# A hybrid decoder trunk on one core: the gated MLP with PSUM chains, seeded down products and one plain pair per layer

## The chip, the core and the metric

The kernel runs on one core of a Trainium2 chip. The time is device microseconds of one launch. Five queues work beside each other and wait for each other through semaphores: TensorE (PE; its weight loads are PEld), VectorE (DVE), ScalarE (ACT), GpSimd (POOL) and SyncE (SP, which here only issues loads from memory). Each works through its own instructions in order.

## The reference

Two layers on 512 tokens of 1024 channels. Layer 0 mixes tokens with a gated recurrence and a pooling branch, layer 1 with a convolution module; each layer then attends to 256 memory tokens and ends with the gated MLP that is changed here. All of it is float32.

```
def conv_ffn(x, norm, w_up, dw_w, dw_b, w_down):
    h = rms_norm(x, norm) @ w_up                       # 1024 -> 2 x 3072
    g = causal_dwconv(h[..., :D_FF], dw_w, dw_b)       # 3 taps along the tokens
    u = h[..., D_FF:]
    return (jax.nn.gelu(g) * u) @ w_down               # 3072 -> 1024
x = x + conv_ffn(...)
```

## The kernel before

Activations stay in SBUF, channels on the partitions and the 512 tokens along a row; the residual is eight tiles X. Every float32 product is three matmuls (mm3): each operand is split into a high part (ScalarE copies it rounded to float32r) and a low part (VectorE subtracts), and high x high, high x low and low x high are summed in PSUM. So each weight block costs a copy on ACT (method high) and a subtraction on DVE (method low).

**The MLP (function ffn, once per layer).** The 3072 hidden channels are 24 chunks of 128. A chunk needs two projections, gate and value: a pair. It is computed in one of two ways.

- *Plain:* two products, each 8 blocks x 3 matmuls of 512 tokens (48 matmuls). The first three chunks are plain (PLAIN = 3), in function opening.
- *Seven products (Strassen's scheme in Winograd's form):* gate and value are the two rows of a 2 x 2 block product, the token halves (256 tokens each) its columns, the channel halves the inner index. Seven products of 4 blocks x 3 matmuls of 256 tokens (84 matmuls) replace eight. The token side (B11, B21, B22 and sums T1 to T4) is made once per layer by class Seven, in four parts; the last part is made in opening. The weight side (a11, a12, a22 and sums s1 to s4) is made per chunk in class Blocks: GpSimd issues DMAs that accumulate within SBUF, on a tile r and a tile z. low() issues each one right behind the low part that last read the tile: r += z after a11, z += a22 after a22, r += a22 after s3, r += a12 after s2. z += a22 has to wait until r += z has landed. s1 is read from z; s3, s2, s4 from r, in this order.

**Function unit(c)** does one chunk: the products in the order a11, a12, s2, s3, s1, s4, a22, each into a PSUM bank of its own (pool of five), then VectorE adds them up (m1, u2, u3, u4, f, g), seven adds of 256 tokens and one copy on ACT. gating() then scales by the norm, convolves three taps, applies gelu, multiplies gate and value and splits the result into ys[c]; it is a generator, so that its later steps are written between the next chunk's. Between the products stand the high and low parts of the next chunks' blocks and the loads (chunk c + 3's first tile, c + 2's second).

**Down products.** The second projection goes in six groups of four chunks. While group g + 1 is computed, each unit does two of the eight output tiles of group g (class Down, 12 matmuls of 512 tokens each, into one of two aux banks); VectorE then adds the bank to X (sum, line 836). The first units of a layer, up to chunk 3, have no down product.

**Function opening** runs the plain chunks. start(0) is the first plain product; then the norm's mean on PE, its root on ACT with a table load, its reciprocal on DVE (scale_of), further plain products, and between them the preparation of the first seven-product chunks (first and second) and the last part of the token sums.

**What sets the order.** Inside ffn the four engines PE, ACT, DVE and POOL run in the order in which the code is written (manual_schedule); SP's loads are placed by a scheduler, which also orders the code around ffn. Each queue waits at its own head: an instruction that waits for a DMA holds up all that is behind it on its engine.

## Time and profile before

| what | value |
|---|---|
| median of 3 runs | 1430.96 us (1429.98 to 1431.38) |
| profiled execution, span | 1429.2 us |
| PE busy, matmuls | 1418.0 us, 99%, 8578 |
| DVE busy | 1184.4 us, 83% |
| ACT busy | 800.7 us, 56% |
| POOL busy | 311.2 us, 22% |
| DMA | 202.23 MB, mean 141 GB/s |

The profile is of one execution. Lines L... are lines of the kernel. "out<-in" names the tile that is written and those that are read; mm and aux are PSUM banks, whi and wlo the high and low parts of weights, raw and wa the tiles that weights are loaded to, bigr other split operands, act split activations. In a timeline a row is start, length, engine, line, operation; in square brackets stands how long the engine sat idle before it, and what ended that. PE's matmuls overlap, so a stage's cost is read from the distance between starts, or from a window that holds whole products. In layer 0 the MLP's first plain product starts at 355.03 us and the first chunk of seven products at 388.16 us.

### The profile page before, as it was taken

The page shows a single profiled execution, that of the slowest core. Times are in us where ns is not written, and L with a number is a line of the kernel's source. Part 1 is how long each engine was busy: PE and PEld are TensorE (multiplying, and loading weights), DVE is VectorE, ACT ScalarE, POOL GpSimd, SP SyncE. Part 2 cuts the span into 40 slices and gives each one's busy share as a digit, 9 for nine tenths or more (in the row PEclk, how much of TensorE's full clock was granted, in tenths as well). Part 3 has the DMA queues.
Part 4 walks back from the last instruction along what each step waited for, and adds up shares of the span by engine and source line. Part 5 has one row for each costly group of instructions (what it writes and reads, how often), then busy time and mean ns, then how long its engine had stood idle before and what let it go on. Part 6 is the DMA issues. An engine that isn't in the chain of part 4 may idle for free.

```text
span 1429.2 us, 22885 instructions
## 1 busy us (share of the span) xinstructions
PE 1418.0 (99%) x8578; PEld 1259.4 (88%) x8578; DVE 1184.4 (83%) x1980; ACT 800.7 (56%) x1336; POOL 311.2 (22%) x325
## 2 busy tenths in 40 slices
PE   9999999999999999999999999999999999999998
PEld 7988888998899999999988777899889999999997
DVE  6987776778888888888888997978788988888885
ACT  7678754666644444544555547767665444444434
POOL 0011310200122221222008992010012222221201
PEclk9999999999999999999999999999999999999999
DMA  8523232542577777777432454345247876877741
GB/s 302 197 74 104 89 119 80 118 111 89 136 183 169 172 181 165 164 176 169 140 119 89 118 158 153 105 87 148 86 114 162 178 184 157 171 183 159 164 127 60
DMA packets 78591, 202.23 MB, mean 141 GB/s; under 512 B 8848, under 2 KB 9360, under 8 KB 78480
## 3 DMA queue, kind: packets, MB, share of 16 engines
q1 hardware_dynamic: 50544, 150.15, 33.6%
q0 software_dynamic: 27648, 50.34, 21.3%
q8 instruction: 67, 1.10, 0.3%
q14 instruction: 44, 0.36, 0.1%
q10 hardware_dynamic: 288, 0.27, 0.1%
HBM read 145.16 MB, written 2.10 MB: 103 GB/s over the span
## 4 chain that ended last, share of the span: by engine, by line
PE 90%; DVE 3%; DMA 2%; POOL 2%; issue 1%; ACT 1%; SPq 0%; POOLq 0%; DVEq 0%; ACTq 0%
PE mm L187 22%; PE mm L186 22%; PE mm L188 22%; PE aux L186 7%; PE aux L187 7%; PE aux L188 7%; PE mm L458 2%; DMA raw<-in_wv 1%; DVE wlo L167 1%; POOL actf L1469 1%; ACT whi L166 1%; PE aux L531 0%; POOL act L167 0%; POOL tmp L1290 0%; DMA raw<-in_pw 0%
## 5 line engine op out<-in xcount | busy, mean ns | idle before, releaser
L187 PE MATMUL mm<-act,whi 128*128 128x512 f32 (+2 forms) x1077 | 377.1, 350 | 0.6 <-DVE act L181 0.5
L188 PE MATMUL mm<-act,wlo 128*128 128x512 f32 (+2 forms) x1077 | 376.7, 350 | 0.0
L186 PE MATMUL mm<-act,whi 128*128 128x512 f32 (+2 forms) x1077 | 376.6, 351 | 0.0
L187 PEld LDWEIGHTS mm<-act,whi 128*128 128x128 f32 x1077 | 203.7, 189 | 29.0 <-DVE act L167 1.0
L186 PEld LDWEIGHTS mm<-act,whi 128*128 128x128 f32 x1077 | 203.4, 189 | 28.4 <-ACT tmp L1468 0.8
L188 PEld LDWEIGHTS mm<-act,wlo 128*128 128x128 f32 x1077 | 203.6, 189 | 25.8
L797 ACT ACTIVATE bigr<-raw 128x512 fp32r<-128x512 f32 x168 | 105.6, 628 | 166.8 <-DMA raw<-wa 70.4
L188 PE MATMUL mm<-bigr,bigr 128*128 128x256 f32 x672 | 190.2, 283 | 0.0
L187 PE MATMUL mm<-bigr,bigr 128*128 128x256 f32 x672 | 190.2, 283 | 0.0
L186 PE MATMUL mm<-bigr,bigr 128*128 128x256 f32 x672 | 190.0, 283 | 0.0
L171 DVE TENSOR_TENSOR tmp<-mm,tmp 128x256 f32<-128x256 f32 x336 | 136.3, 419 | 31.6 <-PE mm L188 25.9
L186 PE MATMUL aux<-act,whi 128*128 128x512 f32 x399 | 156.3, 392 | 0.0
L187 PE MATMUL aux<-act,whi 128*128 128x512 f32 x399 | 156.2, 391 | 0.0
L188 PE MATMUL aux<-act,wlo 128*128 128x512 f32 x399 | 155.2, 389 | 0.0
L804 DVE TENSOR_TENSOR bigr<-raw,bigr 128x512 fp32r<-128x512 f32 x168 | 115.5, 688 | 37.0 <-ACT bigr L797 34.8
L166 ACT ACTIVATE whi<-raw 128x1024 fp32r<-128x1024 f32 (+1 forms) x95 | 96.4, 1019 | 84.1 <-PE mm L187 44.0
L187 PEld LDWEIGHTS mm<-bigr,bigr 128*128 128x128 f32 x672 | 128.9, 192 | 1.6
L186 PEld LDWEIGHTS mm<-bigr,bigr 128*128 128x128 f32 x672 | 128.9, 192 | 1.5
L188 PEld LDWEIGHTS mm<-bigr,bigr 128*128 128x128 f32 x672 | 128.9, 192 | 0.0
L807 POOL DMA_DIRECT2D raw<-raw x48 | 41.6, 866 | 343.1 <-DVE wlo L804 283.3
L811 POOL DMA_DIRECT2D raw<-wa x48 | 41.5, 864 | 308.3 <-DVE bigr L804 258.5
L167 DVE TENSOR_TENSOR wlo<-raw,whi 128x1024 fp32r<-128x1024 f32 (+1 forms) x75 | 90.5, 1210 | 20.0 <-ACT whi L166 19.8
(351 smaller groups left out, 3026.1 us busy)
## 6 DMA issues: line engine op xcount, KB each, us to landing
raw<-wa POOLq DMA_DIRECT2D x144, 256.0 KB, 4.6
wa<-in_wpair SPq DMA_DIRECT2D x84, 256.0 KB, 3.5
raw<-in_wpair SPq DMA_DIRECT2D x42, 512.0 KB, 5.7
big<-in_wdown SPq DMA_DIRECT2D x42, 512.0 KB, 6.7
raw<-raw POOLq DMA_DIRECT2D x48, 256.0 KB, 7.6
raw<-in_pw SPq DMA_DIRECT2D x24, 512.0 KB, 3.4
raw<-in_win SPq DMA_DIRECT2D x20, 512.0 KB, 3.4
raw<-in_wk SPq DMA_DIRECT2D x16, 512.0 KB, 3.6
```

The costliest lines, as they stand in the source:

```text
L166: A.activation(hi, src, AF.Copy)
L167: fetched[1] = (eng or V).tensor_tensor(lo, src, hi.bitcast(F32), op=ALU.subtract)
L171: V.tensor_tensor(out, a, b, op=ALU.add)
L186: PE.matmul(ps, wh, xh, start=first, stop=False)
L187: PE.matmul(ps, wh, xl, start=False, stop=False)
L188: PE.matmul(ps, wl, xh, start=False, stop=last)
L458: PE.matmul(p, m[j], x, start=k == 0 and j == 0 and x is hi, stop=k == C - 1 and x is lo)
L797: A.activation(self.w[name][0], self.block(name), AF.Copy)
L804: V.tensor_tensor(lo, self.block(name), hi.bitcast(F32), op=ALU.subtract)
L807: G.dma_start(self.r, self.z, accum_op=ALU.add)
L811: G.dma_start(self.r, self.a22, accum_op=ALU.add)
L1469: G.tensor_tensor(z[:, s:], z[:, s:], f[:, s:], op=ALU.add)
```

## The change

The weights for one chunk instead of three are laid out plainly (PLAIN = 1), so each layer has 23 chunks of seven products instead of 21.

In a unit the products accumulate in three PSUM banks instead of being added on VectorE. G starts with a11. ScalarE copies G into F (function ahead, done for the next chunk before the present one ends). F then takes s2, s3 and a22, and is copied to SBUF after each; G takes a12; H starts with s1 and takes s4. The order is s1, s2, a12, [down half], s3, [down half], the next chunk's a11, a22, s4. Two adds remain on VectorE. A down half starts on a bank into which ScalarE has copied X, accumulates onto it, and is copied back to X by ScalarE (from chunk 5 on). The opening has two plain products.

```
-PLAIN = 3
+PLAIN = 1
...
-    def mm3(ps, w, x, first, last):
+    def mm3(ps, w, x, first, last, onto=False):
...
+            def bank(self, i, seeded):
+                ps = aux_ps()
+                if seeded:
+                    A.activation(ps, X[2 * self.j + i], AF.Copy)
+                return ps
+            def home(self, i, ps, seeded):
+                if seeded:
+                    A.activation(X[2 * self.j + i], ps, AF.Copy)
+                else:
+                    self.sum(i, ps)
...
-            add(f[:, :M], ps, u3)
+            A.activation(f[:, :M], F, AF.Copy)
+            add(g[:, M:], H, u[:, :M])
...
+        def ahead(c):
+            G, F = main_ps()[:, :M], main_ps()[:, :M]
+            m(c, G, "a11", seven.B11)
+            A.activation(F, G, AF.Copy)
+            return G, F
         def unit(c):
+            G, F = chains
+            down, seeded = downs.get(c), c > GC
+            H = main_ps()[:, :M]
+            m(c, H, "s1", seven.T1)
+            if down:
+                d0 = down.bank(0, seeded)
+            high(c + 1, "s3")
+            m(c, F, "s2", seven.T2, False)
+            u, f, g = tmp_f(), tmp_f(), tmp_f()
+            A.activation(u[:, :M], F, AF.Copy)
+            low(c + 1, "s3")
             next(left, None)
             high(c + 1, "a22")
+            m(c, G, "a12", seven.B21, False)
             next(left, None)
             low(c + 1, "a22")
             next(left, None)
+            if down:
+                down.products(0, d0, seeded)
+                d1 = down.bank(1, seeded)
+            high(c, "s4")
+            low(c, "s4")
+            A.activation(g[:, :M], G, AF.Copy)
+            high(c + 2, "a11")
+            low(c + 2, "a11")
+            m(c, F, "s3", seven.T3, False)
+            if down:
+                down.home(0, d0, seeded)
+            A.activation(u[:, M:], F, AF.Copy)
+            add(f[:, M:], H, u[:, M:])
...
+            if down:
+                down.products(1, d1, seeded)
+            high(c + 1, "s1")
+            low(c + 1, "s1")
+            if c + 1 in pairs:
+                chains = ahead(c + 1)
+            if down:
+                down.home(1, d1, seeded)
+            high(c + 1, "s2")
+            low(c + 1, "s2")
+            m(c, F, "a22", seven.T4, False)
+            m(c, H, "s4", seven.B22, False)
+            left = gating(c, g, f, u, F, H)
...
         def opening():
             start(0)
+            mean = mean_of(ss)
+            high(first, "a11")
+            low(first, "a11")
+            high(first, "a22")
+            low(first, "a22")
+            t = seven.sums(3, lambda: high(first, "a12"))
...
+            high(first, "s3")
+            low(first, "s3")
+            high(first, "s1")
+            low(first, "s1")
+            norm.r = scale_of(mean)
             start(1)
+            high(second, "a11")
+            low(second, "a11")
+            V.tensor_tensor(g, ps[0], norm.r, op=ALU.mult)
+            A.activation(y, g, AF.Identity, scale=dw(2), bias=col("f_dw_b", layer * CF))
+            high(first, "s2")
+            low(first, "s2")
+            chains = ahead(first)
```

How the instructions move at three places. First ACT at the opening of layer 0, before, from the split of the norm's sum on: the table load and root (L306) stand behind the first pair's a11, a22 and a12.

```order
L166 ACTIVATE act_3538<-tmp_3516 128x512
L200 ACTIVATE whi_3569<-raw_3567 128x1024
L797 ACTIVATE whi_3573<-raw_3530 128x512
L797 ACTIVATE bigr_3578<-wa_3533 128x512
L797 ACTIVATE whi_3573<-wa_3532 128x512
L306 ACT_TABLE_LOAD
L306 ACTIVATE tmp_3587<-stat_3584,eps 128x512
L200 ACTIVATE whi_3618<-raw_3616 128x1024
L966 ACTIVATE tmp_3623<-tmp_3621,par 128x512
L797 ACTIVATE bigr_3626<-raw_3530 128x512
```

The same place now, from the first pair's s3 on (raw_3530 is its tile of r and z; mm_3654 and mm_3655 are its G and F, raw_3601 the second pair's tile):

```order
L798 ACTIVATE bigr_3607<-raw_3530 128x512
L798 ACTIVATE bigr_3611<-raw_3530 128x512
L306 ACT_TABLE_LOAD
L306 ACTIVATE tmp_3614<-stat_3569,eps 128x512
L798 ACTIVATE whi_3642<-raw_3601 128x512
L995 ACTIVATE tmp_3540<-tmp_3647,par 128x512
L798 ACTIVATE bigr_3650<-raw_3530 128x512
L892 ACTIVATE mm_3655<-mm_3654 128x256
L798 ACTIVATE bigr_3684<-raw_3601 128x512
L908 ACTIVATE tmp_3698<-mm_3655 128x256
L1004 ACT_TABLE_LOAD
L1004 ACTIVATE tmp_3540<-tmp_3540 128x512
```

The root now stands behind s3 and s1 of the first pair; the copy of G into F (L892) stands behind the root, the Identity (L995) that reads the scaled product, and s2. The copy of F to u (L908) stands behind the second pair's s3.

DVE at the same place, now (L308 is the norm's reciprocal, L994 the scaling of the first plain product by it):

```order
L805 TENSOR_TENSOR bigr_3607<-raw_3530,bigr_3607 128x512
L805 TENSOR_TENSOR bigr_3611<-raw_3530,bigr_3611 128x512
L308 RECIPROCAL r_3616<-tmp_3614 128x512
L805 TENSOR_TENSOR wlo_3643<-raw_3601,whi_3642 128x512
L994 TENSOR_TENSOR tmp_3647<-mm_3538,r_3616 128x512
L805 TENSOR_TENSOR bigr_3650<-raw_3530,bigr_3650 128x512
L805 TENSOR_TENSOR bigr_3684<-raw_3601,bigr_3684 128x512
```

The reciprocal follows the low part of s1 (the second row); the low part of s2 (bigr_3650) comes after it. Before, the reciprocal followed the low part of a12 and stood ahead of the low part of s3.

ACT in a later unit with down halves, now, from the second half's seed on (whi and bigr are weight parts, aux the banks of the down halves):

```order
L838 ACTIVATE aux_5049<-x 128x512
L798 ACTIVATE bigr_5051<-raw_4552 128x512
L922 ACTIVATE tmp_5011<-mm_4928 128x256
L798 ACTIVATE whi_5055<-raw_4904 128x512
L843 ACTIVATE x<-aux_4993 128x512
L929 ACTIVATE tmp_5009<-mm_4929 128x256
L798 ACTIVATE whi_4879<-wa_4906 128x512
L200 ACTIVATE whi_5077<-big_4911 128x1024
L798 ACTIVATE bigr_5101<-raw_4728 128x512
L892 ACTIVATE mm_5105<-mm_5104 128x256
L843 ACTIVATE x<-aux_5049 128x512
L798 ACTIVATE bigr_5120<-raw_4728 128x512
```

Seeds (L838), copies home (L843) and chain copies (L922, L929, L892) now stand among the weight copies; s1 of the next chunk (bigr_5101) stands ahead of that chunk's copy of G into F (L892), and of s2 (bigr_5120).

168 lines of the change are left out of this document (37 added, 131 removed).

## The prediction

> **What bounds the kernel now.** I read the page first, for the span and the chain that ended last, then the windows of the gated MLP, then the timeline of ScalarE (ACT), VectorE (DVE) and GpSimd (POOL) where the MLP of layer 0 opens. The page:
>
> ```profile
> span 1429.2 us, 22885 instructions
> PE 1418.0 (99%) x8578; PEld 1259.4 (88%) x8578; DVE 1184.4 (83%) x1980; ACT 800.7 (56%) x1336; POOL 311.2 (22%) x325
> PE 90%; DVE 3%; DMA 2%; POOL 2%; issue 1%; ACT 1%; SPq 0%; POOLq 0%; DVEq 0%; ACTq 0%
> ```
>
> TensorE (PE) makes up 90% of the chain that ended last. Four stretches of the MLP of layer 0 (first plain product with its mean; the other five plain products; seven half-width products of the first pair without a down matmul; one later pair with its two down halves):
>
> ```profile
> core 0: us, PE busy (x) PEld busy (x) DVE busy (x) ACT busy (x) POOL busy (x), PEclk, DMA share, GB/s
> 355.03:360.48 5.45, 5.45 (x26) 4.51 (x24) 3.43 (x5) 3.56 (x6) 0.00 (x0) 1.00 0.00 0
> 360.94:388.16 27.22, 27.22 (x122) 22.53 (x120) 24.35 (x36) 17.67 (x27) 5.21 (x6) 1.00 0.65 161
> 388.16:398.24 10.08, 10.08 (x86) 10.08 (x85) 9.26 (x18) 4.78 (x10) 2.59 (x3) 1.00 0.72 161
> 477.67:493.23 15.56, 15.56 (x110) 14.58 (x109) 13.43 (x24) 7.28 (x12) 3.47 (x4) 1.00 0.76 170
> ```
>
> PE is busy for the whole of each. So a plain product costs 27.22/5 = 5.44 us, one Strassen product 10.08/7 = 1.44 us (12 matmuls, 0.12 each), a down half (15.56 - 10.08)/2 = 2.74 us. DVE has 13.43 of 15.56 us of work in a pair and PE never waits for it: time taken off DVE there is worth nothing. Only fewer PE cycles shorten the MLP, and only new PE waits lengthen it.
>
> **The change, part by part.**
>
> *Two pairs per layer from plain to seven products.* Two plain products leave (10.89 us) and seven come (10.08): 0.81 us per pair, 3.2 us over four pairs. This is the whole gain.
>
> *Chains and seeds in a steady pair.* Per pair DVE loses five adds and two sums, ACT gains four copies, two seeds and two copies home:
>
> ```profile
> L171 DVE TENSOR_TENSOR tmp<-mm,tmp 128x256 f32<-128x256 f32 x336 | 136.3, 419 | 31.6 <-PE mm L188 25.9 <-ACT bigr L797 2.8
> L886 ACT ACTIVATE tmp<-mm 128x256 f32<-128x256 f32 x42 | 16.0, 380 | 17.8 <-PE mm L188 17.7
> L176 ACT ACTIVATE act<-aux 128x512 fp32r<-128x512 f32 x16 | 8.6, 587 | 0.9 <-PE aux L531 0.9
> ```
>
> ACT gains 4 x 0.38 + 4 x 0.59 = 3.9 us on 7.28 of 15.56: 11.2, still under PE. A copy that writes PSUM does not occur before; I take the 0.38 and 0.59 us of copies that read it (bounds: 0, and the 0.42 us of a DVE add). Each chain copy has another product behind it on PE (1.44 to 2.74 us), so it costs PE nothing. Where a product does wait for such a copy below, it is because ACT works in order and sits in front of something else.
>
> The one tight operand of a steady pair is s1: now the first product, not the fifth. It needs z += a22, a GpSimd accumulate issued after the low part of a22. In the new order that low part waits for the copy of F after the second product (2.9 us into the pair), gelu and the high part: issue at about 5.8 us.
>
> ```profile
> L809 POOL DMA_DIRECT2D raw<-wa x14: 1027/1212/1241, 480.1 to 682.4; - x14
> DMA to landing us min/median/max: 5.1/6.6/8.4
> ```
>
> 5.8 + 6.6 + 0.6 for the high copy = 13.0 against 15.6; at the slowest row, 14.8. No wait in pairs 5 to 23.
>
> *The opening.* Before, six plain products (32.7 us of PE) covered all preparation; now two do, then a11 of the first pair. PE without waits would run: first plain product 355.03 to 360.48, mean to 360.94, second to 366.4, a11 to 367.8, s1 to 369.3, then s2. What those need, by the rows of the same place before (ACT, DVE, POOL):
>
> ```profile
> 358.17 0.63 ACT L166 ACTIVATE act<-tmp 128x512 fp32r<-128x512 f32 x1 [0.96 <-DVE tmp L231]
> 359.65 0.62 ACT L797 ACTIVATE whi<-raw 128x512 fp32r<-128x512 f32 x1
> ...
> 360.70 0.62 ACT L797 ACTIVATE whi<-wa 128x512 fp32r<-128x512 f32 x1
> 361.33 1.28 ACT L306 ACT_TABLE_LOAD   x1
> 362.62 0.69 ACT L306 ACTIVATE tmp<-stat,eps 128x512 f32<-128x512 f32 x1
> 367.59 0.82 ACT L966 ACTIVATE tmp<-tmp,par 128x512 f32<-128x512 f32 x1 [3.33 <-DVE tmp L963]
> ...
> 371.49 0.63 ACT L973 ACTIVATE tmp<-tmp 128x512 f32<-128x512 f32 x1
> ```
> ```profile
> 360.93 0.68 DVE L804 TENSOR_TENSOR wlo<-raw,whi 128x512 fp32r<-128x512 f32 x1
> 361.53 0.69 DVE L804 TENSOR_TENSOR bigr<-wa,bigr 128x512 fp32r<-128x512 f32 x1
> ...
> 363.35 3.35 DVE L308 RECIPROCAL r<-tmp 128x512 f32<-128x512 f32 x1 [0.53 <-ACT tmp L306]
> 366.80 0.69 DVE L963 TENSOR_TENSOR tmp<-mm,r 128x512 f32<-128x512 f32 x1
> ...
> 368.54 1.53 DVE L969 SCALAR_TENSOR_TENSOR tmp<-tmp,par,tmp 128x511 f32<-128x511 f32 x2
> ```
> ```profile
> 361.91 0.86 POOL L807 DMA_DIRECT2D raw<-raw  x1 [70.55 <-DVE wlo L804]
> 368.86 0.86 POOL L809 DMA_DIRECT2D raw<-wa  x1 [6.09 <-DMA raw<-raw]
> ```
> ```profile
> 342.37 18.99 SPq L195 DMA_DIRECT2D raw<-in_wup  x3
> 361.42 0.42 SPq L195 DMA_DIRECT2D big<-in_wdown  x1
> ```
>
> Copies of 512 columns that follow each other start 0.52 us apart on ACT (359.65 and 360.70, two apart), DVE operations 0.60 apart (360.93, 361.53). GpSimd's z += a22 waits for its r += z to land (6.09 us there, beside the last plain load and the down load at 361.4). The new opening has no load at that point (the raw loads of pairs 2 and 3 stand where the first two of the three plain loads stood, and its first down load comes in pair 2), so I use the quiet landings, of the attention stage for r += z and of the late opening for the others:
>
> ```profile
> L807 POOL DMA_DIRECT2D raw<-raw x3: 855/855/1010, 240.2 to 277.6; - x3
> DMA to landing us min/median/max: 3.3/3.4/3.6
> L809 POOL DMA_DIRECT2D raw<-wa x1: 1004/1004/1004, 385.1 to 385.1; - x1
> DMA to landing us min/median/max: 4.3/4.3/4.3
> L815 POOL DMA_DIRECT2D raw<-wa x1: 862/862/862, 384.4 to 384.4; - x1
> DMA to landing us min/median/max: 3.3/3.3/3.3
> ```
>
> First wait, s1: a11's high copy right behind the 358.17 row (358.7), low to 360.1, r += z lands 363.6, z += a22 issued 363.7 lands 368.0, high copy to 368.7, low 0.69 later, which the third matmul needs: PE waits 0.9 + 0.5 = **1.4 us** (5.2 at 6.7 and 5.0 us of landing).
>
> Second wait, s2, the largest: the norm's root now stands on ACT behind s1's high copy, and F's seed copy stands behind what needs that root. Table load 368.6 to 369.9, root 370.55, reciprocal 3.35 to 373.95, low part of the second pair's a11 0.60, product with r 0.69 to 375.2, Identity 0.82 to 376.0, s2's high copy 0.52, F's copy 0.38: 376.9. PE is done with s1 at 370.65: **6.3 us**, with s2's low part 6.5. No DMA is in this one. Before, the same reciprocal ran to 366.7 under plain product two.
>
> Third wait, the sixth product (a22): it needs F copied to u after s3. On ACT that copy is behind much. The second pair's s3 waits for its r += z, which goes out only after 374.6 and lands at 378.1: copied to 378.8. DVE takes its low part and the plain pair's two convolution steps (0.60 + 1.53) before gelu, 381.1 to 381.7, and two products (1.3) before the result's copy at 383.1. Then s4, g's copy, a11 (0.52 + 0.29 + 0.52) and u's copy, 384.9 to 385.3. PE, with four products from 377.1, is there at 382.9: **2.4 us**.
>
> Fourth, pairs 2 to 4 come after units of only 10.1 us, without down products. In such a unit z += a22 goes out about 7.0 us after s1 starts (s1, s2, u's copy, gelu, a22's copy and low part) and, landed, needs 0.6 for the high copy and 0.5 beyond it for the low part; PE is back at s1 after 10.1, the 0.5 of its own s1 and 0.9 for a late u (below): late by landing time - 3.4, so 0.9 us at 4.3, 3.2 at 6.6, 5.0 at 8.4. I take 4.8 us for pair 2 (few loads beside it) and 6.5 and 6.8 for 3 and 4 (loads as in the steady units): 1.4 + 3.1 + 3.4 = **7.9**. An ACT that is blocked by s1 comes late with u once each in pairs 2 and 3: 0.9 each, **1.8**.
>
> Sum per layer 1.4 + 6.5 + 2.4 + 7.9 + 1.8 = 20.0 us, 40.0 for two. All later PE work is dense, so nothing is won back. 1429.2 - 3.2 + 40.0 = 1466.0 by the span. The runs' median, 1430.96, is 1.8 above that span: **1468 us**.
>
> A rule beside the table-load row: the Trainium skill ("ScalarE: Activation LUTs", What ACT_TABLE_LOAD costs) puts a switch of sets at about 2.66 us, load plus drain. The row has 1.28, starting as the copy of 360.70 ends; the trace does not agree. By the page the second wait would be 1.4 us longer, and the sum an estimated 3 us higher.
>
> **The rivals.**
>
> *Loaded landings (1478).* If loads do lie beside the first pair's accumulates, the 361.91 row counts (landed 368.6): s1 5.2, s3 of the first pair 2.3 more behind the second pair's r += z, a22 3.3. That is 25 us per layer even with 5 us in pairs 2 to 4: 1431 - 3 + 50. For it: DMA share 0.65 in the second window. Against it: those are loads the new opening has already made.
>
> *Slow s1 in every steady pair (1492).* If z += a22 lands later than about 9 us, each of some 20 pairs per layer waits 0.6 us: 24 us more. The slowest steady row is 8.4.
>
> *The clock (1473).* The 6.3 us hole may cost clock after it. The end of the kernel is the only place before with PE idle for long:
>
> ```profile
> 1415.00:1429.00 14.00, 7.50 (x59) 7.08 (x57) 7.32 (x20) 5.75 (x17) 4.39 (x5) 0.84 0.40 151
> ```
>
> PE is busy half of that window and the granted clock falls to 0.84 of it. At half clock for 5 us behind the hole PE would lose some 2.5 us, of which the third wait (2.4 us, set by ACT) takes up most; I give 0 to 2 us per layer. The Trainium skill ("TensorE: Matmul & The Clock Gate", Why this matters for your kernels) says that an idle gap of over about 3 us drops the clock to half; by it the drop is likely here, and the row does not contradict it.
>
> *PE stays fed (1428).* The gain of 3.2 us stands alone if the waits total under 1.6 us per layer. That is decided at one place, F's seed copy: it would have to be done by 369.3. What speaks for it is only that PE waits nowhere in the opening now; against it, the reciprocal alone is 3.35 us and stands behind s1.
>
> **How the numbers follow.** Forecast 0.52 (1462 to 1475), loaded landings 0.18, clock 0.16, slow s1 0.09, PE stays fed 0.05. Range 1454 to 1488: below it the quietest landings everywhere (15.6 us per layer, 1459) less 5 for copies that cost less than I took; above it loaded landings with the clock. It leaves out fed PE and slow s1. 0.2% is 2.9 us, about what a measurement of this kernel tells from no change: faster 0.05, same 0.02, slower 0.93.
>
> **What would show it.** In the profile after, PE idle of 6 us before an s2 product, named as a wait for the ACT copy into mm, once per layer, with the reciprocal right before it; a wait of 1 to 5 us before the first s1, for ACT's copy; waits of 2 to 4 us before each of the next three s1 products; steady pairs still 15.56 us with ACT near 11 us; plain window of 5.44 us unchanged. I am wrong if the span from the first plain product to pair 5 grows by under 10 us over its PE work, or if steady pairs leave 15.56 us.

## The result

| | before | after |
|---|---|---|
| median of 5 runs each | 1431.03 us (1429.98 to 1431.81) | 1489.91 us (1484.75 to 1496.47) |
| ratio, 95% interval | 1 | 1.0417 (1.0392 to 1.0442) |
| profiled execution: time, span | 1430.96 us (median then), 1429.2 us | 1494.74 us, 1492.9 us |

The change makes the kernel 4.2% slower. The forecast was 1468 us and the range 1454 to 1488: the direction was right, the loss is 59 us instead of 37, and the time lies 1.9 us above the range's upper end. The profiled run is one of the longer ones; what follows splits its 63.7 us of span.

### The profile after

The page, answering to the three lines of before:

```profile
span 1492.9 us, 23101 instructions
PE 1444.3 (97%) x8722; PEld 1281.3 (86%) x8722; DVE 1092.4 (73%) x1722; ACT 935.5 (63%) x1696; POOL 324.6 (22%) x341
PE 57%; DMA 18%; DVE 10%; ACT 7%; issue 6%; POOL 3%; SPq 0%; POOLq 0%; ACTq 0%; DVEq 0%
```

PE's share of the chain fell from 90% to 57%, and DMA rose from 2% to 18%: TensorE now waits for others. The windows tell where. The five stretches are: layer 0 from its first plain product to its first down half; on to the end of the MLP's products; on to the plain product of layer 1; and the same two of layer 1. First after, then before (whose layer 1 takes the same 48.95 and 305.45 us):

```profile
354.46:425.28 70.82, 56.04 (x351) 52.23 (x350) 46.18 (x72) 37.37 (x71) 15.17 (x18) 0.86 0.58 127
425.28:736.60 311.32, 308.63 (x2115) 286.00 (x2114) 212.35 (x313) 200.79 (x390) 64.68 (x75) 1.00 0.69 163
736.60:1073.39 336.79, 332.83 (x1805) 275.02 (x1803) 286.17 (x488) 210.19 (x362) 120.57 (x93) 0.99 0.40 117
1073.39:1145.89 72.50, 57.13 (x352) 53.23 (x350) 46.09 (x72) 37.35 (x71) 14.73 (x17) 0.86 0.58 124
1145.89:1460.33 314.44, 310.50 (x2115) 286.28 (x2113) 211.73 (x312) 199.42 (x387) 65.18 (x75) 1.00 0.69 160
```
```profile
355.04:403.99 48.95, 48.95 (x279) 43.24 (x278) 42.33 (x64) 29.86 (x48) 7.99 (x10) 1.00 0.59 140
403.99:709.44 305.45, 305.45 (x2115) 285.81 (x2113) 264.20 (x456) 142.67 (x238) 65.11 (x75) 1.00 0.74 169
709.44:1041.91 332.47, 330.31 (x1803) 273.88 (x1802) 283.34 (x482) 207.51 (x356) 120.66 (x93) 1.00 0.40 116
```

The second number of a row is the stretch in us, the next PE's busy time, the third from the end the granted clock. The openings with the units that have no down half grew by 21.9 and 23.6 us, the later pairs by 5.9 and 9.0, the work between the layers by 4.3; the rest shrank by 0.9. Before, PE was busy for all of its MLP; now it is not, and the clock in the openings is 0.86.

The waits of TensorE's weight loads, as groups (engine, tile, line, then who was waited for: us in total, times, longest):

```profile
PEld mm L186 <- ACT bigr L798: 16.0, 10, 4.7
PEld mm L186 <- ACT mm L892: 12.4, 2, 6.2
...
PEld aux L186 <- ACT act L881: 5.8, 7, 0.9
PEld mm L188 <- DVE bigr L805: 5.6, 15, 0.4
PEld mm L186 <- ACT tmp L929: 4.7, 4, 2.3
PEld aux L187 <- DVE act L883: 4.1, 8, 0.5
```

L892 is the copy of G into F: once per layer, 6.2 us. L798 and L805 are the high and low parts of weight blocks (s1 above all), L929 the copy of F to u after s3, L881 and L883 the split of a gated tile, for which a down half waits.

The hole of layer 0 on PE, and ACT in front of it:

```profile
376.03 0.58 PE L186 MATMUL mm<-bigr,bigr 128*128 128x256 f32 x1 [5.99 <-ACT mm L892]
376.41 0.41 PE L187 MATMUL mm<-bigr,bigr 128*128 128x256 f32 x1
376.62 0.45 PE L188 MATMUL mm<-bigr,bigr 128*128 128x256 f32 x1
```
```profile
367.18 0.63 ACT L798 ACTIVATE bigr<-raw 128x512 fp32r<-128x512 f32 x1 [2.89 <-DMA raw<-wa]
367.83 1.28 ACT L306 ACT_TABLE_LOAD   x1
369.13 0.69 ACT L306 ACTIVATE tmp<-stat,eps 128x512 f32<-128x512 f32 x1
...
374.38 0.81 ACT L995 ACTIVATE tmp<-tmp,par 128x512 f32<-128x512 f32 x1 [4.04 <-DVE tmp L994]
375.10 0.61 ACT L798 ACTIVATE bigr<-raw 128x512 fp32r<-128x512 f32 x1
375.61 0.36 ACT L892 ACTIVATE mm<-mm 128x256 f32<-128x256 f32 x1
```

Copy of F at 375.61, s2 at 376.03: the prediction's second wait, row by row. Behind it the matmuls of 256 columns start 0.21 us apart (376.41 and 376.62) instead of 0.12: half clock. The window of 10.2 us that begins in the hole, and the next:

```profile
372.00:382.20 10.20, 6.17 (x28) 6.17 (x29) 5.14 (x7) 4.38 (x7) 3.48 (x4) 0.50 0.48 75
382.20:392.50 10.30, 8.91 (x74) 8.71 (x74) 8.86 (x15) 6.76 (x15) 1.72 (x2) 1.00 0.76 183
```

In all, the execution spent 47.8 us at half clock, before 6.9 (at its end).

### The profile page after: what moved, and what is told of

Same layout as the page of the kernel before. It is cut to its first block, busy times and chain, and to the rows that moved or that the text cites. A ratio compares the mean times of both kernels' runs of the same rounds, so it can differ in the third digit from the quotient of the medians.

```text
span 1492.9 us, 23101 instructions
## 1 busy us (share of the span) xinstructions
PE 1444.3 (97%) x8722; PEld 1281.3 (86%) x8722; DVE 1092.4 (73%) x1722; ACT 935.5 (63%) x1696; POOL 324.6 (22%) x341
## 4 chain that ended last, share of the span: by engine, by line
PE 57%; DMA 18%; DVE 10%; ACT 7%; issue 6%; POOL 3%; SPq 0%; POOLq 0%; ACTq 0%; DVEq 0%
DMA raw<-wa 16%; PE mm L188 14%; PE mm L186 14%; PE mm L187 14%; PE aux L187 4%; PE aux L188 4%; PE aux L186 3%; DVE bigr L805 3%; PE mm L458 2%; DVE tmp L875 2%; ACT tmp L871 2%; DVE tmp L870 1%; ACT bigr L798 1%; DMA raw<-raw 1%; POOL raw L812 1%
## 5 line engine op out<-in xcount | busy, mean ns | idle before, releaser
L186 PE MATMUL mm<-act,whi 128*128 128x512 f32 (+2 forms) x1045 | 362.2, 348 | 2.5 <-ACT act L274 1.5
L187 PE MATMUL mm<-act,whi 128*128 128x512 f32 (+2 forms) x1045 | 363.1, 347 | 0.2
L188 PE MATMUL mm<-act,wlo 128*128 128x512 f32 (+2 forms) x1045 | 362.5, 347 | 0.0
L805 DVE TENSOR_TENSOR bigr<-raw,bigr 128x512 fp32r<-128x512 f32 x184 | 126.8, 690 | 162.9 <-ACT bigr L798 162.4
L186 PE MATMUL mm<-bigr,bigr 128*128 128x256 f32 x736 | 215.2, 292 | 29.9 <-ACT bigr L798 13.8
L186 PEld LDWEIGHTS mm<-act,whi 128*128 128x128 f32 x1045 | 199.0, 191 | 28.8 <-ACT act L274 2.0
L187 PEld LDWEIGHTS mm<-act,whi 128*128 128x128 f32 x1045 | 199.3, 191 | 26.2 <-DVE act L167 1.0
L188 PEld LDWEIGHTS mm<-act,wlo 128*128 128x128 f32 x1045 | 199.2, 191 | 23.3
L188 PE MATMUL mm<-bigr,bigr 128*128 128x256 f32 x736 | 215.6, 293 | 2.4 <-DVE bigr L805 2.4
L187 PE MATMUL mm<-bigr,bigr 128*128 128x256 f32 x736 | 212.8, 289 | 0.0
L798 ACT ACTIVATE bigr<-raw 128x512 fp32r<-128x512 f32 x184 | 114.1, 620 | 143.5 <-DMA raw<-wa 138.6
L186 PEld LDWEIGHTS mm<-bigr,bigr 128*128 128x128 f32 x736 | 146.0, 198 | 34.9 <-ACT bigr L798 16.0
L188 PEld LDWEIGHTS mm<-bigr,bigr 128*128 128x128 f32 x736 | 145.6, 198 | 6.0 <-DVE bigr L805 5.6
L187 PEld LDWEIGHTS mm<-bigr,bigr 128*128 128x128 f32 x736 | 146.1, 198 | 1.7
L808 POOL DMA_DIRECT2D raw<-raw x52 | 45.0, 864 | 384.2 <-DVE wlo L805 367.4
L816 POOL DMA_DIRECT2D raw<-wa x52 | 44.8, 861 | 319.2 <-DVE bigr L805 277.6
L167 DVE TENSOR_TENSOR wlo<-raw,whi 128x1024 fp32r<-128x1024 f32 (+1 forms) x75 | 90.4, 1210 | 18.9 <-ACT whi L166 18.7
L186 PEld LDWEIGHTS aux<-act,whi 128*128 128x128 f32 x399 | 75.3, 189 | 18.9 <-ACT act L881 5.8
```

Of the source, the lines that this page charges most:

```text
L167: fetched[1] = (eng or V).tensor_tensor(lo, src, hi.bitcast(F32), op=ALU.subtract)
L186: PE.matmul(ps, wh, xh, start=first, stop=False, skip_group_check=onto)
L187: PE.matmul(ps, wh, xl, start=False, stop=False, skip_group_check=onto)
L188: PE.matmul(ps, wl, xh, start=False, stop=last, skip_group_check=onto)
L798: A.activation(self.w[name][0], self.block(name), AF.Copy)
L805: V.tensor_tensor(lo, self.block(name), hi.bitcast(F32), op=ALU.subtract)
```

## The experiments

Theory A: the short opening and the units without down halves cost some 23 us per layer, and the later pairs lose by s1's late weights. Rivals: the chains as such (B), the opening alone (C), the clock as a loss of its own or not (A against D), accumulates slowed by other DMA traffic (E). All times are medians of four runs (ten for the mended version with three plain pairs); each ratio is to runs of the kernel before made beside them, whose medians are 1430.8 to 1431.5 us.

### The units alone, and the opening alone

Three plain pairs, the opening of before, the new units:

```
-PLAIN = 1
+PLAIN = 3
     def opening():  # of before, ending in
+            left = rest()
+            chains = ahead(first)
```

> Three plain pairs per layer with the opening of the kernel before, but the new units (PSUM chains, seeded down halves, s1 first). Theory A (the short opening and the units without down halves carry the loss, some 23 us per layer of the 59 in all): what is left is the loss of the later pairs, 5.9 and 9.0 us by the changed kernel's stages, and 4.3 between the layers; 1431 + 19 = 1450 us, 1445 to 1455, and no half-clock stretch in the trace before the end. Theory B (the chains are at fault: each unit now needs copies that ScalarE makes late): the loss stays mostly where it is, 1470 or more. Theory C (the units are free, all of it is the opening): 1431 to 1435.

Measured: **1454.0 us**, ratio 1.0161 (1.0142 to 1.0180). Layer 0, opening and later pairs:

```profile
354.69:403.64 48.95, 48.95 (x279) 43.23 (x278) 39.63 (x57) 30.17 (x50) 7.79 (x9) 1.00 0.58 140
403.64:718.31 314.67, 310.16 (x2114) 286.05 (x2113) 212.53 (x314) 201.04 (x391) 65.30 (x75) 1.00 0.69 162
```

This is in theory A's range. The opening is before's to the hundredth, with no half clock. The later pairs lose 9.2 us (10.5 in layer 1). So 23 us of the 59 come with the units where the opening is long. What the short opening costs by itself is the next run; the two need not add up.

One plain pair and the short opening, with the units of before:

```
-PLAIN = 3
+PLAIN = 1
     def opening():  # of after, without
-            chains = ahead(first)
     def unit(c):    # of before
```

> One plain pair per layer with the short opening of the changed kernel, but the units of the kernel before (a bank of its own for each product, sums on VectorE, s1 fifth, no seeds). Theory A: the hole before s2 stays, since s2's high copy still stands behind the root, the 3.35 us reciprocal and the Identity; 4 to 6 us per layer with a stretch of half clock behind it; no wait of pairs 3 and 4 for s1 (s1 is the fifth product there, some 7 us later in the pair than as first), and later pairs of 15.56 us: 1431 - 3 + 2 x (6 + 3) = 1446, 1438 to 1452. Theory B (the chains are at fault): 1428 to 1432.

Measured: **1470.8 us**, 1.0275 (1.0259 to 1.0291), above both ranges.

```profile
377.80 0.58 PE L186 MATMUL mm<-bigr,bigr 128*128 128x256 f32 x1 [7.20 <-ACT bigr L797]
```
```profile
356.21:423.56 67.35, 54.45 (x351) 51.03 (x350) 49.56 (x85) 31.67 (x55) 14.74 (x17) 0.87 0.62 134
423.56:729.00 305.44, 304.66 (x2109) 284.63 (x2108) 264.89 (x456) 145.74 (x243) 65.31 (x75) 1.00 0.74 168
```

Without chains and seeds the hole is there too, 7.2 us, now for s2's high copy, which stands behind the same reciprocal and Identity. The later pairs take 305.4 us as before. Theory B falls for the opening: two plain products are too short a cover for either kind of unit. Theory A's place for the loss is right, its size is not: it counted the hole and some half clock, 9 us per layer, but the weight loads of TensorE wait 14.3 and 14.0 us in the two openings, half of it for high and low parts behind the hole, and the openings are 18.4 us longer than before's. By itself the short opening costs 40 us net of the 3.2 us that it saves PE, so it is the larger part of the loss; 40 and 23 are 4 us more than the 59 of both together.

### The accumulate z += a22

High and low part of the next pair's a22 ahead of its s3:

```
+            high(c + 1, "a22")
+            low(c + 1, "a22")
             high(c + 1, "s3")
             m(c, F, "s2", seven.T2, False)
...
-            high(c + 1, "a22")
             m(c, G, "a12", seven.B21, False)
-            low(c + 1, "a22")
```

> The changed kernel with one thing moved in each unit: the high and low parts of the next pair's a22, and with them GpSimd's z += a22, stand ahead of that pair's s3 instead of behind it, so that z += a22 goes out some 4 to 5 us earlier. Theory A (s1 waits for the landing of z += a22): the waits before s1 of the third and fourth pair (4.6 + 2.0 us in layer 0, 4.0 + 3.2 in layer 1) and their half-clock stretches go, and the waits of 0.3 to 0.8 us before s1 in later pairs: 1490 - 14 - 8 - 6 = 1462, 1457 to 1470. Theory E (the accumulates are limited by the DMA traffic beside them, or ScalarE by its order, so the wait only shifts to s3 or to the copy of F): 1480 or more.

Measured: **1471.2 us**, 1.0275 (1.0256 to 1.0295): 18.7 us less than after, 1.2 us above theory A's range. One later pair, and then ScalarE's high copies from raw in the whole kernel, first after, then here (busy, mean ns, idle just before them, by whom):

```profile
491.90:507.46 15.56, 15.56 (x111) 14.58 (x110) 10.74 (x16) 10.26 (x22) 3.47 (x4) 1.00 0.70 164
```
```profile
L798 ACT ACTIVATE bigr<-raw 128x512 fp32r<-128x512 f32 x184 | 114.1, 620 | 143.5 <-DMA raw<-wa 138.6 <-DMA raw<-raw 5.0
```
```profile
L798 ACT ACTIVATE bigr<-raw 128x512 fp32r<-128x512 f32 x184 | 114.2, 621 | 16.2 <-DMA raw<-wa 10.2 <-DMA raw<-raw 5.4 <-PE mm L188 0.5
```

In the changed kernel ScalarE stood 138.6 us at the head of its queue, at s1's high copy, until an accumulate landed; F's copy, the copies to u and the gated tile are behind it. With a22 first it is 10.2 us and every pair within a group takes 15.56 us. What is left is the gated tile at the first down half of a group, 0.4 us each time and 1.2 + 0.5 at the first of a layer.

The same edit with three plain pairs:

> The run with three plain pairs and the new units (1454.0), with the next pair's a22 and its z += a22 ahead of s3 in each unit. Theory A (what is left in the later pairs, 9.2 and 10.5 us per layer, is s1 late by the landing, and a gated tile that is late for the first down half of each group, 0.4 to 1.2 us five times per layer): the s1 part goes, the group part stays near the 0.4 to 0.5 us that it had with a22 first: 1454 - 14 = 1440, 1437 to 1444, later pairs of 15.56 us. Theory E (DMA traffic): 1450 or more.

Measured: **1441.1 us**, 1.0070 (1.0055 to 1.0085), as theory A has it: 13 of the units' 23 us were this accumulate.

But why was it late? One line of the changed kernel moved, the low part of s3 behind that of a22:

```
             A.activation(u[:, :M], F, AF.Copy)
-            low(c + 1, "s3")
             next(left, None)
...
             low(c + 1, "a22")
+            low(c + 1, "s3")
```

> The changed kernel (1489.9) with one line moved: the low part of the next pair's s3, and with it r += a22, stands behind the low part of a22 instead of ahead of it. In the changed kernel GpSimd issues z += a22 0.54 us behind r += a22, which is as large, and it lands after 8.0 us (median of 18, 4.5 to 9.4); with a22 first it went out 4.1 us earlier and with nothing beside it, and landed after 4.4 (4.1 to 5.9). Theory Q (it lands late because the other accumulate is ahead of it): z += a22 still goes out 6.5 to 7 us behind the F copy, but lands after 4 to 6 us, r += a22 takes the 8; the later pairs come to 15.56 us plus the groups' gated tile, and the time to that of a22 first or a little above: 1468 to 1477. Theory E (the loads at that moment slow it, or the 4 us of earlier issue were what counted): landing of 7 us or more, waits before s1 as before, 1483 to 1492.

Measured: **1480.2 us**, 1.0343 (1.0326 to 1.0361), between the two ranges. GpSimd and VectorE in a pair of the changed kernel (L812 is r += a22, L810 z += a22, L816 r += a12; on VectorE bigr<-raw is here the low part of s3, bigr<-wa that of a22):

```profile
506.86 0.86 POOL L812 DMA_DIRECT2D raw<-wa  x1 [3.52 <-DVE bigr L805]
507.40 1.21 POOL L810 DMA_DIRECT2D raw<-wa  x1
```
```profile
505.58 0.69 DVE L805 TENSOR_TENSOR bigr<-raw,bigr 128x512 fp32r<-128x512 f32 x1
...
507.03 0.69 DVE L805 TENSOR_TENSOR bigr<-wa,bigr 128x512 fp32r<-128x512 f32 x1
```

and in the experiment:

```profile
515.26 0.86 POOL L816 DMA_DIRECT2D raw<-wa  x1 [5.69 <-DVE bigr L805]
515.79 1.21 POOL L810 DMA_DIRECT2D raw<-wa  x1
522.50 0.86 POOL L812 DMA_DIRECT2D raw<-wa  x1 [5.50 <-ACT bigr L798]
```
```profile
520.67 0.69 DVE L805 TENSOR_TENSOR bigr<-wa,bigr 128x512 fp32r<-128x512 f32 x1
```

z += a22 goes out at 515.79, 4.9 us *before* the low part of a22 runs: it never waited for it, both only read a22. What held it in the changed kernel is GpSimd's order: it stands behind r += a22, which waits for the low part of s3 (3.52 us in the row). So the theory's premise that it would go out at 6.5 to 7 us was wrong; it went out 2.9 us behind the start of the F copy (median of 18), as with a22 first, against 7.0 in the changed kernel. Its landing (first line after, then this run, each 18 issues of layer 0's later pairs):

```profile
DMA to landing us min/median/max: 4.5/8.0/9.4
```
```profile
DMA to landing us min/median/max: 4.1/4.4/5.6
```

In both it follows another accumulate by 0.54 us, so an accumulate ahead of it does not by itself make the 8 us. What differs is the traffic: DMA share 1.00 in the 8 us behind the issue in the changed kernel, 0.79 in the 4.4 us here:

```profile
507.40:515.40 8.00, 8.00 (x56) 7.43 (x55) 4.74 (x7) 4.96 (x10) 2.07 (x3) 1.00 1.00 245
```
```profile
515.79:520.20 4.41, 4.41 (x38) 4.37 (x37) 3.30 (x6) 2.93 (x6) 1.22 (x2) 1.00 0.79 138
```

The trace of the changed kernel speaks for the loads, with the neighbour the same: behind the issue at 712.12 the loads (queue q1) take 21% of the DMA engines in the next 4.4 us, and it lands after 4.5 us; at 507.40 they take 59%, and it lands after 7.5; at 570.73 77%, and 8.0. Of the 37 issues of both layers' later pairs, those with more than 55% of loads landed after 8.1 us at the median, the two with less than 30% after 4.5. This is still no experiment: no run moved the loads alone. And they are not all of it. In the kernel before, where r += a22 stands ahead too, the issue at 480.13 had 3% of loads behind it and took 6.4 us. There and in the changed kernel the two accumulates read the same tile, a22; in this run they don't. No run tested that either. The later pairs are mended as with a22 first (15.56 us); what this run takes longer than that one lies in the openings, 69.8 and 68.2 us against 64.3 and 60.9.

### The clock

Extra a11 products where PE idled, ahead of the first s1 and of those of pairs 3 and 4:

```
-            chains = ahead(first)
+            chains = ahead(first, 5)      # a11 five times
...
+            for _ in range({first + 2: 3, first + 3: 1}.get(c, 0)):
+                m(c, G, "a11", seven.B11)
             m(c, H, "s1", seven.T1)
```

> The changed kernel with extra products that repeat a11 of the same pair into the same bank, with the same result: four more in the opening ahead of s1 and s2 (5.8 us of TensorE work where it now idles 6.2 us), three more ahead of the third pair's s1 (4.3 us where it idles 4.6) and one ahead of the fourth's (1.4 where it idles 2). It takes no wait away, it only keeps TensorE busy in it. Theory A (the half clock is a loss of its own that the idle stretch brings, 47.8 us at half clock against 6.9 before; about 7 us per layer): half-clock stretches behind these holes vanish and the time falls by 10 to 16 us, to 1475 to 1480. Theory D (the half clock lies over waits that ScalarE and the accumulating DMAs set anyway): the stretches vanish but the time stays within 3 us, 1487 to 1493.

Measured: **1490.7 us**, 1.0428 (1.0395 to 1.0461), no gain, though half clock fell from 47.8 to 23.4 us. The median is in theory D's range, but the runs lie between 1481 and 1497, and in the profiled one, the shortest, the openings take 68.7 and 68.1 us against 70.8 and 72.5. So this alone decides little. With a22 first the runs are closer (1468.4 to 1472.8), and there only the opening's hole was filled:

> The run with a22 first (1471.2), with a11 of the first pair made five times instead of once, into the same bank with the same result: TensorE then works through the 6.1 us in which it waited for s2, and the wait itself is as long as before. Nothing later is moved. Theory A (the half clock behind the hole is a loss of its own, 7 to 10 us at half clock per layer, 3.4 to 5 us of time): 1471 - 2 x 4 = 1463, 1460 to 1466. Theory D (what follows the hole ends with the copy of F to u before a22, which ScalarE reaches at the same moment whatever the clock; the wait before a22 only grows from 2.5 to 4 us or so, and may bring a half-clock stretch of its own): 1469 to 1473, with the a22 product at the same distance from the opening.

Measured: **1472.8 us**, 1.0288 (1.0273 to 1.0304). Theory D. Layer 0's opening to the first down half, with a22 first and with the hole filled too:

```profile
354.12:418.46 64.34, 53.08 (x351) 49.11 (x350) 44.45 (x69) 36.33 (x69) 15.32 (x18) 0.92 0.62 138
```
```profile
354.30:418.55 64.25, 56.82 (x400) 53.10 (x398) 44.27 (x69) 36.23 (x69) 15.51 (x18) 0.97 0.63 138
```

The clock rises from 0.92 to 0.97 and the stretch stays the same: the products behind the hole end earlier and then wait longer before a22 (4.0 us instead of 2.5) for a copy that ScalarE reaches at the same moment. The half clock behind the hole costs nothing by itself there. In layer 1 the opening even got longer, 64.5 us against 60.9: the wait before a22 grew from 2.1 to 4.1 us, and 6.83 us at half clock came behind it, where the run with a22 first had none behind that wait. So the half clock is not free everywhere; it is where a later wait for ScalarE takes up what the matmuls lose. For the half clock behind the s1 waits of pairs 3 and 4 (5.2 and 3.4 us of matmuls in layer 0, so at most 4.3 us) this stays open.

### The gated tile of a group's first down half

With a22 first, the first down half moved behind s3:

```
-            if down:
-                down.products(0, d0, seeded)
-                d1 = down.bank(1, seeded)
             high(c, "s4")
...
             m(c, F, "s3", seven.T3, False)
+            if down:
+                down.products(0, d0, seeded)
+                d1 = down.bank(1, seeded)
             A.activation(u[:, M:], F, AF.Copy)
...
```

The half's copy home to X moves behind the copy to u with it.

> The changed kernel with a22 first (1471.2), and the first down half moved from ahead of s3 to behind it, so that the gated tile of the pair before has 1.44 us more. Theory A (at the first pair of each group the first down half waits for that tile: 0.4 us four times and 1.2 + 0.5 once per layer): 1471 - 5 = 1466, 1463 to 1468. Rival: s3 adds onto F, which has to be copied to u first, and only a12 (1.44 us) then stands between s2 and s3; if ScalarE does not get to that copy within 1.4 us, every pair waits 0.2 to 1 us: 1475 to 1510.

Measured: **1466.1 us**, 1.0245 (1.0228 to 1.0262), theory A. From the first down half of layer 0 on, PE does not wait at all:

```profile
420.86:724.46 303.60, 303.60 (x2102) 284.43 (x2101) 207.43 (x311) 199.62 (x389) 64.40 (x74) 1.00 0.71 166
```

### The order of the opening

The prediction said the hole is decided at one place, F's seed copy. With a22 first, that copy and s2 ahead of the root:

```
-            norm.r = scale_of(mean)
             start(1)
+            chains = ahead(first)
+            high(first, "s2")
+            low(first, "s2")
+            norm.r = scale_of(mean)
             high(second, "a11")
...
-            high(first, "s2")
-            low(first, "s2")
-            chains = ahead(first)
```

> The changed kernel with a22 first (1471.2), and in the opening the copy of G into F and the first pair's s2 ahead of the root instead of behind root, reciprocal, scaling and Identity. Nothing else is moved. The prediction's statement (the 6.3 us are decided at one place, F's seed copy): the wait before s2 falls from 6.1 us to under 1 and its half clock goes, 1471 - 2 x (5 to 8) = 1455 to 1461. Theory F (the seed copy is only the first of several things behind the root: F's next copy, to u, stands behind the second pair's s3, whose r += z goes out only after the reciprocal): the hole moves from before s2 to before s3, 7 to 8 us there, the sixth product starts where it did, and the time stays at 1468 to 1474.

Measured: **1475.5 us**, 1.0308 (1.0293 to 1.0323): 4 us worse than with a22 first, 1.5 above theory F's range.

```profile
379.80 0.58 PE L186 MATMUL mm<-bigr,bigr 128*128 128x256 f32 x1 [6.80 <-ACT tmp L910]
```
```profile
375.88 0.81 ACT L997 ACTIVATE tmp<-tmp,par 128x512 f32<-128x512 f32 x1 [4.04 <-DVE tmp L996]
...
378.84 0.63 ACT L798 ACTIVATE bigr<-raw 128x512 fp32r<-128x512 f32 x1 [1.63 <-DMA raw<-raw]
379.38 0.37 ACT L910 ACTIVATE tmp<-mm 128x256 f32<-128x256 f32 x1
```

The mechanism is theory F's: the hole moved two products on, to s3, which waits for F's next copy, to u (L910). That copy is behind the Identity (L997), which waits 4.04 us for the reciprocal, and behind the second pair's s3.

So the whole order has to change. With a22 first: root where ScalarE waited for a DMA anyway, reciprocal behind s1, the plain pair's gating in the first unit:

```
             high(first, "s3")
             low(first, "s3")
+            high(second, "a11")
+            low(second, "a11")
+            A.activation(sd, mean, AF.Sqrt, bias=eps)
             high(first, "s1")
             low(first, "s1")
+            V.reciprocal(norm.r, sd)
             start(1)
+            chains = ahead(first)
...
+            high(second, "a22")
+            low(second, "a22")
```

> The changed kernel with a22 first (1471.2), and the opening in another order: the plain products go to the two aux banks; the second pair's a11 right behind the first pair's s3; the root ahead of s1, where ScalarE sat idle for 2.9 us on a DMA; the reciprocal behind s1's low part; F's copy, s2 and the second pair's a22 right behind; scaling and Identity of the plain pair in the first unit behind the copy of F to u, its convolution, gelu and products at the end of that unit. By the rows of the run with a22 first: s1 0.8 us late, s2 0.3 to 0.8, s3 0, a22 0 to 1, the second unit's s3 1 to 2: some 4 us of waits per layer and no hole of over 3 us, so no half clock, against 14 us of waits and 7 to 10 us at half clock now: 1471 - 2 x 8 = 1455, 1450 to 1461. Rival (ScalarE and VectorE have too much to do in the two units without down halves, so the same work only comes late elsewhere): 1465 or more.

Measured: **1464.7 us**, 1.0231 (1.0216 to 1.0247), above the range, almost at the rival's 1465.

```profile
372.95 0.39 PE L188 MATMUL mm<-bigr,bigr 128*128 128x256 f32 x1 [2.11 <-DVE bigr L805]
391.51 0.58 PE L186 MATMUL mm<-bigr,bigr 128*128 128x256 f32 x1 [4.09 <-ACT tmp L912]
```

The 6 us before s2 are 2.1 now (its low part is behind the reciprocal); 4.1 come back in the second unit, behind the plain pair's gelu and products. Both were taken up next, with the first down half behind s3 and the plain pair's gating spread over the second and third unit:

```
+            high(first, "a11")
+            low(first, "a11")
+            high(first, "a22")
+            low(first, "a22")
             ss = split(norm.ss)
...
-            V.reciprocal(norm.r, sd)      # now in the first unit, behind s3's low part
...
             add(f[:, M:], H, u[:, M:])
+            if c in (second, second + 1):
+                next(zero)                # a step of the plain pair's gating
```

> One plain pair and the new units, with all that the runs pointed to: a22 first; the first down half behind s3; first a11 and a22 ahead of the norm's sum split; root ahead of s1; the reciprocal moved from ahead of the low part of s2 (2.27 us of wait in the reordered opening) to the first unit, behind s3's low part; the plain pair's gating in the second and third unit instead of at the end of the first (it cost the second unit's s3 4.3 and 5.5 us). By the rows of the reordered opening: s1 0.5, s2 0.5, later 1 to 2 us: first plain product to first down half 49 to 52 us against 66 with the half moved and 47.4 of TensorE work, no hole above 3 us there and no half clock; 303.6 us for the rest of the MLP: 354.5 + 50.5 + 303.6 + 336 + 50.5 + 303.6 + 32.8 + 1.8 = 1433, 1429 to 1440. Rival (the two engines cannot prepare the units without down halves in 10.1 us each, whatever the order): 1445 or more.

Measured: **1446.4 us**, 1.0102 (1.0085 to 1.0119), above the range and in the rival's. The opening of layer 0:

```profile
354.85:411.20 56.35, 50.82 (x363) 47.22 (x362) 45.20 (x72) 35.92 (x69) 14.71 (x17) 1.00 0.73 160
```

No half clock any more in the openings, but 7.6 us over the 48.8 of PE work (47.35, and 1.44 for the s3 ahead of the half; 8.2 in layer 1). VectorE is busy for 45 of those 56 us: in units of 10.1 us on PE it has the high and low work of a whole pair, the gating, and the plain pair besides. In the waits of this run PE waits for copies of F to u (6.4 and 3.9 us in all) and for low parts (4.1). That no order could do better, as the rival says, is not shown: neither ScalarE (36 us) nor VectorE is busy all the time.

And three plain pairs, with a22 first and the first down half behind s3:

> Three plain pairs and the new units with a22 first (1441.1), and the first down half behind s3. Theory A (the waits of the first down halves for a gated tile are the last of the later pairs, 2 to 3 us per layer): the MLP's later part 303.6 us per layer as in the run with one plain pair, 1.8 less than before's 305.45, 1441 - 2 x 5 = 1431 plus what differs between the layers, 1429 to 1436. Rival: 1438 to 1442.

Measured: **1434.6 us**, 1.0024 (1.0015 to 1.0033), in theory A's range. The MLP is nearly level with before now: 51.7 + 303.6 and 50.8 + 303.6 us in the two layers, against 48.95 + 305.45. (The split between the two parts moved, since s3 now stands ahead of the first down half.) Of the profiled run, one of the longest of the ten at 1437.1 us, most of what is left lies between the layers, 336.3 us against 332.5. It is the best version of the new units and still 3.2 us slower than before: with three plain pairs they take nothing off PE, and PE is the bound.

## Why the prediction was right, and where it was wrong

- **Bound, and PE work.** Right. TensorE's work was all there was to gain: with every wait gone PE is busy for all 303.6 us of the later pairs.
- **Steady ScalarE load, near 11 us.** 10.26 of 15.56 us in the pair shown with a22 first; the chain copies into F cost 0.37 us and the seeds 0.58, as the rows of copies that read PSUM said.
- **First wait, 1.4.** 0.6 and 0.4 us in layer 0, 0.6 in layer 1.
- **Second wait, 6.3 with 6.5.** 6.15 and 0.26 us (layer 1: 6.14, 0.26). The chain of rows was right to a quarter of a microsecond; the table load in it took 1.28 us, as in the row of before, and the root followed at once.
- **"That is decided at one place, F's seed copy."** Wrong. With the seed copy early the hole moved to s3 and the time rose by 4 us. Everything on ScalarE behind the root was late, not one copy.
- **Third wait, 2.4.** 1.6 and 2.3 us.
- **Fourth wait, 7.9 and 1.8 per layer.** Too much by some 2 us in sum, and that near only by luck, for it is wrong inside: pairs 2, 3, 4 lost 0.4, 4.9 and 2.3 us in layer 0 (0.3, 4.2, 3.5 in layer 1), forecast 1.4, 3.1, 3.4 and 1.8 for u. Pair 2's s1 did not wait at all; its 0.4 is before a22. The step "z += a22 goes out ... a22's copy and low part" named the wrong holder: it waits behind r += a22 in GpSimd's order, and that one for s3's low part. The landing of pair 3 was 9.2 us against the 6.5 taken.
- **The clock, 0 to 2 us per layer.** The second term that was too small; the sum itself had nothing for it. (The rival's 1473 is 5 us over the forecast, more than the 0 to 2 per layer beside it.) There were 20.5 us at half clock per layer, in several stretches. The waits in the openings are 16.6 and 17.3 us of the 23.5 and 25.2 over PE's 47.35; the other 6.9 and 7.9 fit the matmuls that ran at half clock there, 14.8 and 17.3 us of busy PE, half of which is 7.4 and 8.7. That the third wait takes up what follows the big hole was right for layer 0 (64.25 us against 64.34). The Trainium skill ("TensorE: Matmul & The Clock Gate", Why this matters for your kernels), with its drop to half clock after an idle gap of over about 3 us, is confirmed for the gaps of 6.2 and 4.6 us, but the runs show the drop after shorter ones too (2.3 us, last section): where they differ, the runs decide. So the waits before pair 4's s1 (1.9 + 0.4 us in layer 0) and before layer 1's first a22 (2.3) brought half clock of their own, which the prediction hadn't reckoned with.
- **"No wait in pairs 5 to 23", the step that failed most.** It made the sum 14.9 us too small (5.9 and 9.0). The sum 5.8 + 6.6 + 0.6 = 13.0 of 15.56 us was too small in two terms: counted from s1's first matmul, z += a22 went out after 6.1 and 6.4 us (medians of the two layers), and it landed after 8.0 more in layer 0 (9.4 at most, where the row of before had 6.6 and 8.4), so 14.2 and 15.0 us into the pair, 16.1 at most. The loss has two parts. The accumulate did not merely make s1 late: it stopped ScalarE at s1's high copy, and all that is behind it. And the first down half of each group now stands ahead of s3 and waits for the gated tile, 0.5 + 0.65 us each time in the changed kernel, 0.4 once ScalarE isn't stopped. By the distances between matmul starts the waits for s1's parts are some 6 us of the 14.9, those of the down halves some 8. The prediction looked only whether s1 itself would be in time. Its own sign of being wrong, steady pairs that leave 15.56 us, came. The rival *slow s1 in every steady pair* has the place, at a smaller price.
- **Between the layers: no term, 4.3 us.** PE there waits for the new norm (1.5 us idle before the projection's first product, 1.0 for the last gated tile), with 3.4 us of half clock behind. Before, 35 matmuls of 256 columns stood between the norm's token sums and that projection; now 16 do, the others run earlier. A scheduler places them, and no run tested it.

By terms of the profiled run: forecast span 1466.0; waits of the openings 6.1 less than the 40, half clock in the openings 14.7, later pairs 14.9, between the layers 4.3, the rest -0.9: 1492.9, as measured. So the terms that failed are those that stood at nothing: the waits of the later pairs, the clock, and the work between the layers.

## What to carry to other kernels

Follow the engine, not the operand: when an in-order engine stops at its head for a transfer, price everything queued behind it, not only the consumer of that transfer; and read who really holds an issue from its data and its place in its queue, not from the line of code it was written behind. A hole that comes from a serial chain (root, reciprocal, scaling, Identity) moves when one consumer is taken out of it; it shrinks when the chain is put where its engines were idle (6.2 us before s2 became 2.1, with 4.1 elsewhere). And a change that frees an engine with slack (VectorE, 1184 to 1092 us) while the bound stays cannot win more than the bound's own saving, here 3.2 us; in the best version with one plain pair the new waits of one opening alone, 7.6 us, are more than that.

## What the runs showed of the hardware

- Half clock came in stretches of 3.41 us or multiples (3.41, 6.83, 10.24), and short waits were enough for it. In the reordered opening the 2.27 us before s2 (2.11 of idle in the row shown there) were followed by one; here two windows of 3.41 us, the wait being in the first:

```profile
369.92:373.33 3.41, 1.30 (x11) 1.10 (x10) 3.41 (x3) 1.10 (x2) 0.14 (x1) 1.00 0.40 94
373.33:376.74 3.41, 3.41 (x19) 3.41 (x18) 1.36 (x3) 1.23 (x3) 2.50 (x3) 0.50 0.66 109
```

  The 2.5 us before a22 with a22 first and 1.9 + 0.4 us before pair 4's s1 in the changed kernel brought one too. The length of a wait does not decide it: in the mended version with one plain pair 1.50 + 0.2 us of idle between the layers brought a stretch, waits of up to 1.9 us in its openings did not. What does fit is how much PE was busy in the 3.41 us that end where a stretch starts: 1.71 us at 750.86 in that version. A window of the same length in the run with a22 first, up to 1096.67 and on the grid of its stretches, had 1.73 us busy and none followed. Over the traces of all the versions, from the first MLP on, each such window with 1.8 us of idle or more was followed by half clock, and none with under 1.4 us was unless it lay in such a stretch itself; between the two it went either way. No run varied this alone.
- An accumulating DMA of 256 KB from one SBUF tile to another landed after 3.2 to 9.9 us over all the traces. Neither its size nor an accumulate 0.54 us ahead of it tells which; the share of loads behind it goes with it (21%: 4.5 us, 59%: 7.5, 77%: 8.0 in the changed kernel).
- The spread from run to run was larger where ScalarE waited on accumulates, 1484.8 to 1496.5 us for the changed kernel, than with a22 first, 1468.4 to 1472.8. That these waits make it is not shown.
